# Seven small edits to a one-core encoder step: a later column norm, stored second parts on VectorE, wider biased blocks in the long-range attention, and unit-matrix transposes at the start

## The chip, the cores and the metric

The kernel runs on one core of one Trainium2 chip. The metric is the device time of one execution in microseconds; the kernel before was run three times, and the median counts. Engines are called as the profile calls them: PE (TensorE, the matrix engine), DVE (VectorE), ACT (ScalarE), POOL (GpSimd) and SP (SyncE, which here issues every transfer).

## What is computed

One layer of a streaming encoder, for 2048 prompt tokens and 32 sample tokens of 1024 features, all in float32. The parts that matter here:

```python
qa, ka, va, qb, kb, vb = split_proj(rmsnorm(hp, g_attn[i]), w_in[i])
oa = diff_attn_prompt(qa, ka, va, t5_table, lam)     # 4 heads, two maps each, all earlier keys
ob = band_attn_prompt(qb, kb, vb, band_table[i])     # 8 heads, the last 9 chunks of 64
hp = hp + merge(oa, ob, subln_g[i], out_norm_b[i], w_out[i], lam_init)
hp = ffn_ple(hp, p_prompt[i], g_mlp[i], w_up[i], w_down[i], w_ple_gate[i], w_ple_proj[i])

def diff_core(q, k, v, bias, mask, lam):
    s = jnp.einsum('bqhmd,bkhmd->bhmqk', q, k).astype(jnp.float32) * (HEAD_DIM ** -0.5) + bias[:, None]
    s = jnp.where(mask, s, NEG)
    p = jax.nn.softmax(s, axis=-1)
    w = p[:, :, 0] - lam * p[:, :, 1]
    return jnp.einsum('bhqk,bkhe->bqhe', w.astype(v.dtype), v)

def ffn_ple(h, p, g_mlp, w_up, w_down, w_ple_gate, w_ple_proj):
    c = rmsnorm(h, g_mlp)
    h = h + jnp.square(jax.nn.relu(c @ w_up)) @ w_down
    return h + jax.nn.sigmoid(h @ w_ple_gate) * (p @ w_ple_proj)
```

The bias of the long-range attention differs only for keys less than 128 positions away; further back it is one constant per head, which the kernel subtracts from the table, so that those keys need no bias at all.

## The kernel before

**Numbers in two parts.** Every matrix operand is split into a rounded first part and the rest, its second part (`split`, L181 to L187: the first part by ACT, the second by POOL through `pool_tt`, L166 and L176, or by DVE, L187). `mm3` (L216 to L218) multiplies two such operands with three matmuls. Weights come by `wunit`: one transfer, then a split, by default on ACT and POOL.

**Tokens** go in four blocks of 512 (block 3 has 544, with the samples). `prep` normalises and transposes a block (PE L378 `xp`, ACT L383, DVE L384), `vtile` and `proj` make values, queries and keys (`vps`, `qps`). The order of the stages is: projections of blocks 0 and 1; long-range attention over tiles 0 to 7 (`attn_a` with `JA0`) together with the projections of the band group; band attention (`attn_b`); projections of blocks 2 and 3; long-range attention over tiles 8 to 15 and the samples (`JA1`) together with output projections and the MLP of blocks 0 and 1; then `gate` and `final` of block 1, the output projections of blocks 2 and 3, and the MLP of blocks 2 and 3 in a form with seven products instead of eight (`mlp7`, whose input parts come from `cparts` for block 2 and from `cstage` and `cload`, by way of device memory, for block 3).

**Order.** The program doesn't run in the order in which it is written. A scheduler with a model of the engines fixes, when the program is built, the order of the instructions on each engine; a stage written earlier has priority, and later work fills the gaps. On the chip each engine takes its instructions strictly in that order, so one that waits holds up all behind it. "Filler" below is matmul work of another stage that stands between those of the attention. Generators woven together by `weave` and `weave2` set the written order.

**Long-range attention** (`attn_a_pair`). For each head and pair of tiles of 128 queries, the keys of a tile are cut into blocks: far ones up to 512 wide without bias and a last one of at most 256 with bias. Per block and map: two matmuls into `s` (L633), then for a far block the negated maximum (`nm`, DVE L639), for the last block one DVE operation that adds the bias `ba` and takes the maximum (L642) and a second that turns its sign (L645), then the exponential with its sum on ACT (L647). When there are several blocks, their maxima are brought together (L652 to L659) and the factors `c` of both maps made (L660, L661). ACT multiplies map 1 by its factor (L669) and DVE adds map 0 to it (L670). PE transposes the result (`tpp`, L705), ACT and DVE split it (L712, L713), and PE multiplies it with the values (`o`, L719 to L721). A norm over each head follows: `ss` on PE (L730, L731), then ACT, four steps on POOL (L227 to L231), `os` on DVE (L733) and the store `oT`. The bias tile has one buffer; POOL fills a masked corner of it (L330) once its transfer is there.

**Around block 2's MLP.** The output projection of block 3 (`ops`) is woven with `cparts` of block 2. Its squares are summed on POOL in `sqacc`. Then the gate of block 0 is begun (`hu`: the split of `h`; `gps`, `pps`: its products), and `colnorm` of block 3 follows in the written order: `sh` on ACT, `sl` on DVE, the sums over features on PE (`css`, L1087, L1088), then three ACT and four DVE steps. Its result `r3` is used by `cstage`, which makes the seven input parts of block 3, one eighth for each of the chunks of block 2's MLP from the fifth on, after `final` of block 0 has had four. Of the second parts of an eighth (`cst`) DVE makes all but one, POOL the parts `b11` and `t4`.

Of the kernel before, what the change touches and what calls it, by code (L numbers as in the profile page):

```python
# [13 lines left out]
F32 = mybir.dt.float32  # L14
# [129 lines left out]
class Kern:  # L144
# [125 lines left out]
    def lam(self, cp, wk):  # L270
        nc, a = self.nc, self.a
        lv = wk.tile([P, 4, HD], F32, name="lv")
        for i, n in enumerate(("lambda_q1", "lambda_k1", "lambda_q2", "lambda_k2")):
            self.dma(lv[:, i], a[n].broadcast_to([P, HD]))
        pr = wk.tile([P, 2, HD], F32, name="lpr")
        nc.vector.tensor_tensor(pr[:, 0], lv[:, 0], lv[:, 1], op=ALU.mult)
        nc.vector.tensor_tensor(pr[:, 1], lv[:, 2], lv[:, 3], op=ALU.mult)
        s = wk.tile([P, 2], F32, name="lsum")
        nc.vector.tensor_reduce(s, pr, axis=AX.X, op=ALU.add)
        e = wk.tile([P, 2], F32, name="lexp")  # L280
        nc.scalar.activation(e, s, AF.Exp)
        self.nlam = cp.tile([P, 1], F32, name="nlam")
        nc.vector.tensor_tensor(self.nlam, e[:, 1:2], e[:, 0:1], op=ALU.subtract)
        nc.vector.tensor_scalar(self.nlam, self.nlam, -LAM_INIT, None, op0=ALU.add)
# [40 lines left out]
    def bias_a(self, pool, h):  # L325
        nc = self.nc
        t = pool.tile([P, 256], F32, tag="ba", bufs=1, name="ba")
        src = self.dba[h, 127 : 127 + P * 383].rearrange("(p c) -> p c", c=383)[:, :256]
        self.dma(t, src)
        nc.gpsimd.memset(t[0:64, 192:256], NEG)  # L330
        return t
# [259 lines left out]
    def attn_a_pair(self, g, j, kt, ba, pool, ps_s, ps_t, ps_o):  # L591
# [11 lines left out]
        for qi, t in enumerate(tiles):  # L603
            if samp:
                nr = SS
                blocks = [(SP, PAST + SS, 0)]
# [22 lines left out]
            for bi, (k0, n, near) in enumerate(blocks):  # L629
                for m in range(2):  # L630
# [7 lines left out]
                    if near is None:  # L638
                        nc.vector.tensor_reduce(nmx, s, axis=AX.X, op=ALU.max, negate=True)  # L639
                        src = s  # L640
                    else:
                        nc.vector.tensor_tensor_reduce(  # L642
                            dst, s, ba[:nr, near : near + n], 1.0, -3e38, ALU.add, ALU.max, nmx
                        )
                        nc.vector.tensor_scalar(nmx, nmx, -1.0, None, op0=ALU.mult)  # L645
                        src = dst
                    nc.scalar.activation(dst, src, AF.Exp, bias=nmx, accum_out=z[:nr, m, bi : bi + 1])  # L647
            c = pool.tile([P, 2, 8], F32, tag="c", bufs=2, name="c")
            rz = pool.tile([P, 2], F32, tag="rz", bufs=2, name="rz")
            if nb > 1:  # L650
                gm = pool.tile([P, 2], F32, tag="gm", bufs=2, name="gm")
                nc.vector.tensor_reduce(gm[:nr], nm[:nr, :, :nb], axis=AX.X, op=ALU.min)  # L652
                for m in range(2):
# [6 lines left out]
                nc.vector.tensor_scalar(c[:nr, 0, :nb], c[:nr, 0, :nb], rz[:nr, 0:1], None, op0=ALU.mult)  # L660
                nc.vector.tensor_scalar(  # L661
                    c[:nr, 1, :nb], c[:nr, 1, :nb], rz[:nr, 1:2], self.nlam[:nr], op0=ALU.mult, op1=ALU.mult
                )
            else:
                nc.vector.reciprocal(c[:nr, :, 0], z[:nr, :, 0])
                nc.vector.tensor_scalar(c[:nr, 1, 0:1], c[:nr, 1, 0:1], self.nlam[:nr], None, op0=ALU.mult)
# [363 lines left out]
    def cstage(self, b, up, out, r):  # L1030
# [5 lines left out]
        for k in range(4):  # L1036
# [18 lines left out]
            parts(("b11", "pool"), ("b21", "dve"), ("b22", "dve"))  # L1055
# [5 lines left out]
            parts(("t2", "dve"), ("t1", "dve"), ("t3", "dve"), ("t4", "pool"))  # L1061
# [241 lines left out]
    def gate(self, b, h, up, act, md, wk=None):  # L1303
# [3 lines left out]
        pT = [[up.tile([P, BLK], F32R, tag="u", name="pT") for _ in range(2)] for _ in range(2)]  # L1307
# [14 lines left out]
        for dq in range(2):  # L1322
# [3 lines left out]
            for d4 in range(4):  # L1326
                d = 4 * dq + d4
                wh, wl = self.wunit(Wg[:, P * d : P * d + P].rearrange("(k p) c -> p k c", p=P), [8, P])
                for s0, sn in SUBS[b]:
# [6 lines left out]
                        up.tile([P, BLK], F32, tag="u", name="sig") if wk is None  # L1336
# [29 lines left out]
    def final(self, b, h, up, fk, mm, md=None):  # L1366
# [5 lines left out]
        def side(c0, tn, q):  # L1372
# [8 lines left out]
            if phased and q == 1:  # L1381
                yns[c0, q] = yp
            else:
                yns[c0, q] = up.tile([P, BLK], F32, tag="u", name="yn")[:, :512]
# [4 lines left out]
            junk = up.tile([P, BLK], F32, tag="u", name="junk")[:tn, :512]  # L1389
# [8 lines left out]
        def emit(c0, tn, r):  # L1398
            tt = t0 + c0
            dst = a["y_prompt"][0, tt : tt + tn] if tt < SP else a["y_sample"][0, tt - SP : tt - SP + tn]  # L1400
            for q in range(2):
                src = yn = yns[c0, q]
                if phased and q == 1:
                    yn = up.tile([P, BLK], F32, tag="u", name="yo")[:, :512]
# [24 lines left out]
    def run(self):  # L1429
        tc, nc, a = self.tc, self.nc, self.a  # L1430
        with ExitStack() as top:
# [24 lines left out]
            with ExitStack() as x:  # L1456
# [7 lines left out]
                def first():  # L1464
                    self.consts(cp)

# [4 lines left out]
                units.append(self.vunits(0, 0, pool=wv))  # L1471
                next(gen)
# [136 lines left out]
            r3 = self.colnorm(acc[3][0], 3, 1.0 / D, wk, mm, "mm", None)  # L1609
# [6 lines left out]
            h = box[0]  # L1616
            parts = {}
# [63 lines left out]
```

## Time and profile before

| | us |
|---|---|
| median of three runs | 3172.29 |
| the three runs | 3168.67, 3172.29, 3180.61 |
| profiled execution | 3175.31 |
| its span in the trace | 3173.5 |
| PE busy in the span | 3019.3 (95%) |
| DVE, ACT, POOL busy | 1889.9 (60%), 1878.7 (59%), 1843.7 (58%) |

The profile is of one execution. Busy time is the time in which an engine had at least one instruction under way; PE's matmuls overlap, so the times of single matmuls add up to more than that. In a row of a group, `out<-in` names the tiles (buffer numbers left out), "x768" counts the instructions, then come the total busy time in us, the mean of one in ns, and the idle time of the engine ahead of them with what ended it. A row of the waits reads: engine, tile and line that waited, what ended the wait, us in total, times, longest. A row of the timeline reads: start in us, duration in us, engine, line, operation. A row of the stretches gives, for each window, its length, then the busy time of PE, of PE's weight loads, of DVE, ACT and POOL with the instructions counted, the granted clock of PE as a share, the busy share of the transfer engines and GB/s.

### The profile page before, as it was taken

Reading aid. Unit: us, or ns where it says so; the run is one execution under the profiler, and the core shown is the slowest. Engines: PE = TensorE matmul, PEld = TensorE weight load, DVE = VectorE, ACT = ScalarE, POOL = GpSimd, SP = SyncE. Lnnn points to the kernel's source line nnn. Section 1 sums busy time; section 2 is a strip of 40 time slices with the busy share of each in tenths; the row PEclk is TensorE's granted clock in tenths of the full one; section 3 lists DMA queues with packets and bytes.
Section 4 is the critical chain, followed back from the end, with each engine's and each line's share of the span. In section 5 each row is a group of like instructions: output and inputs, shape, how many; then the busy total and the mean of one; then the engine's idle time right before and its main releaser. Section 6 shows DMA issues by size and latency. Waiting matters only on the chain.

```text
span 3173.5 us, 52785 instructions
## 1 busy us (share of the span) xinstructions
PE 3019.3 (95%) x17913; PEld 2656.2 (84%) x17913; DVE 1889.9 (60%) x4588; ACT 1878.7 (59%) x4166; POOL 1843.7 (58%) x2504
## 2 busy tenths in 40 slices
PE   8999898999999999999999999999799999999998
PEld 7787787899987887878788788878588888999998
DVE  5157774645465654676756656535667775476653
ACT  5257775765676764766666557454555455554545
POOL 2447455332345544655555545677777888767674
PEclk9999999999999999999999999999899999999999
DMA  8788757976788745555663543537433446333231
GB/s 278 243 245 244 206 181 227 261 228 200 211 243 233 210 126 151 155 151 152 173 176 116 141 118 108 160 118 231 129 126 120 151 135 232 122 102 112 87 115 56
DMA packets 522134, 537.17 MB, mean 169 GB/s; under 512 B 38620, under 2 KB 401440, under 8 KB 521864
## 3 DMA queue, kind: packets, MB, share of 16 engines
q1 hardware_dynamic: 521864, 533.80, 57.0%
q8 instruction: 142, 2.33, 0.3%
q14 instruction: 128, 1.05, 0.1%
HBM read 419.88 MB, written 117.75 MB: 169 GB/s over the span
## 4 chain that ended last, share of the span: by engine, by line
PE 68%; DMA 12%; DVE 8%; ACT 4%; POOL 3%; issue 3%; SPq 1%; DVEq 0%; POOLq 0%; ACTq 0%
PE dps L216 6%; PE dps L218 6%; PE ups L216 6%; PE dps L217 6%; PE ups L217 6%; PE ups L218 6%; PE qps L216 3%; PE qps L217 3%; PE qps L218 3%; PE s L633 3%; PE gps L216 2%; PE gps L217 2%; PE gps L218 2%; PE ob L877 2%; PE sb L825 2%
## 5 line engine op out<-in xcount | busy, mean ns | idle before, releaser
L176 POOL TENSOR_TENSOR wl<-wr,wh 128x256 fp32r<-128x256 f32 x648 | 473.1, 762 | 355.2 <-ACT wh L181 332.6
L181 ACT ACTIVATE piece<-wr 128x512 fp32r<-128x512 f32 x406 | 246.4, 625 | 285.8 <-PE ups L217 112.1
L176 POOL TENSOR_TENSOR piece<-wr,piece 128x256 fp32r<-128x256 f32 x404 | 327.0, 835 | 102.0 <-ACT piece L181 93.1
L181 ACT ACTIVATE wh<-wr 128x1024 fp32r<-128x1024 f32 x228 | 241.1, 1058 | 180.2 <-PE qps L217 42.7
L166 POOL TENSOR_TENSOR wl<-wr,wh 128x256 fp32r<-128x256 f32 x264 | 199.7, 787 | 193.7 <-ACT wh L181 187.2
L218 PE MATMUL dps<-uh,piece 128*128 128x272 f32 (+1 forms) x768 | 248.8, 326 | 5.7 <-POOL piece L166 5.6
L216 PE MATMUL dps<-uh,piece 128*128 128x272 f32 (+1 forms) x768 | 246.7, 325 | 5.3 <-ACT piece L181 3.9
L217 PE MATMUL dps<-ul,piece 128*128 128x272 f32 (+1 forms) x768 | 248.2, 324 | 0.0
L216 PE MATMUL ups<-cs,piece 128*128 128x256 f32 (+1 forms) x864 | 246.3, 286 | 1.1 <-DVE r L1219 1.0
L218 PE MATMUL ups<-cs,piece 128*128 128x256 f32 (+1 forms) x864 | 245.5, 284 | 0.0
L217 PE MATMUL ups<-cs,piece 128*128 128x256 f32 (+1 forms) x864 | 245.4, 284 | 0.0
L166 POOL TENSOR_TENSOR piece<-wr,piece 128x256 fp32r<-128x256 f32 x280 | 230.3, 852 | 23.9 <-ACT piece L181 20.9
L216 PE MATMUL qps<-aH,wh 128*128 128x512 f32 (+1 forms) x640 | 232.5, 363 | 7.3 <-ACT kn L506 4.3
L218 PE MATMUL qps<-aH,wl 128*128 128x512 f32 (+1 forms) x640 | 230.3, 360 | 0.0
L217 PE MATMUL qps<-aL,wh 128*128 128x512 f32 (+1 forms) x640 | 229.8, 359 | 0.0
L1208 DVE TENSOR_TENSOR h<-h,dps 128x272 f32<-128x272 f32 (+1 forms) x384 | 189.6, 514 | 58.5 <-PE dps L218 57.8
L1160 DVE TENSOR_TENSOR h<-h,dps 128x512 f32<-128x512 f32 x256 | 174.3, 682 | 78.7 <-PE dps L218 73.5
L216 PE MATMUL dps<-uh,wh 128*128 128x512 f32 x512 | 209.0, 408 | 12.2 <-DVE h L1160 6.9
L633 PE MATMUL s<-ka,q 128*128 128x512 f32 (+3 forms) x768 | 187.4, 345 | 18.4 <-ACT e L647 8.0
L216 PE MATMUL ups<-cH,wh 128*128 128x512 f32 x512 | 203.0, 397 | 1.5 <-ACT cH L181 1.1
L218 PE MATMUL dps<-uh,wl 128*128 128x512 f32 x512 | 202.1, 395 | 0.5 <-POOL wl L166 0.4
L218 PE MATMUL ups<-cH,wl 128*128 128x512 f32 x512 | 201.9, 394 | 0.0
(315 smaller groups left out, 9635.7 us busy)
## 6 DMA issues: line engine op xcount, KB each, us to landing
wr<-w_up SPq DMA_DIRECT2D x128, 512.0 KB, 3.9
wr<-w_down SPq DMA_DIRECT2D x128, 512.0 KB, 3.8
wr<-w_in SPq DMA_DIRECT2D x74, 512.0 KB, 5.4
q<-qS SPq DMA_DIRECT2D x128, 256.0 KB, 5.4
v<-vSa SPq DMA_DIRECT2D x64, 512.0 KB, 3.7
ka<-kS SPq DMA_DIRECT2D x32, 512.0 KB, 8.9
wr<-w_out SPq DMA_DIRECT2D x32, 512.0 KB, 4.7
wr<-w_ple_gate SPq DMA_DIRECT2D x32, 512.0 KB, 4.4
```

The lines of the kernel that those rows point to most:

```text
L166: nc.gpsimd.tensor_tensor(out[:, sl], a[:, sl], b[:, sl], op=op)
L176: nc.gpsimd.tensor_tensor(out[:, sl], a[:, sl], b[:, sl], op=op)
L181: nc.scalar.activation(hi, raw, AF.Copy)
L216: nc.tensor.matmul(ps, lh, rh, start=start and i == 0, stop=False)
L217: nc.tensor.matmul(ps, lh, rl, start=False, stop=False)
L218: nc.tensor.matmul(ps, ll, rh, start=False, stop=stop and i == n - 1)
L633: nc.tensor.matmul(s, q[:, m, hl, P * qi : P * qi + nr], kt[:, m, k0 - kb : k0 - kb + n], start=hl == 0, stop=hl == 1)
L825: ins = nc.tensor.matmul(s, q[:, hl, P * qi : P * qi + nr], kt[:, c : c + w], start=hl == 0, stop=hl == 1)
L877: nc.tensor.matmul(o[:, :, qa:qb], vt, p[:kn, i - kfirst, :, qa:qb], start=x == 0, stop=x == len(order) - 1)
L1160: nc.vector.tensor_tensor(hv, hv, ps, op=ALU.add)
L1208: nc.vector.tensor_tensor(hv, hv, ps, op=ALU.add)
```

## The change

Seven edits:

1. `colnorm` of block 3 moves from ahead of block 2's MLP to behind its first two steps.
2. In `cstage` the second parts of `b11` and `t4` are made by DVE instead of POOL, so that POOL makes none there.
3. In the long-range attention the last, biased block of a tile takes up to 512 keys instead of 256. The bias tile is 512 wide, its first half filled with zeros by POOL. Tiles 2, 3, 6, 7, 10, 11, 14 and 15 have one block fewer.
4. The biased block's operation gives the negated scores and their minimum, so that the separate change of sign goes, and the exponential takes a scale of −1.
5. The factors of both maps are made together, with a vector that holds 1 and −lambda (`lamv`) in place of `nlam`.
6. PE transposes the unit matrix 14 times once it is written, and 20 times behind the first tile's transposes. The results aren't used.
7. In `gate` and `final` the tiles of the pool `up` take the pool's width (`up.aw`, 512 for blocks 0 and 1) instead of 544.

```diff
     def bias_a(self, pool, h):
         nc = self.nc
-        t = pool.tile([P, 256], F32, tag="ba", bufs=1, name="ba")
+        t = pool.tile([P, 512], F32, tag="ba", bufs=1, name="ba")
+        nc.gpsimd.memset(t[:, :256], 0.0)
         src = self.dba[h, 127 : 127 + P * 383].rearrange("(p c) -> p c", c=383)[:, :256]
-        self.dma(t, src)
-        nc.gpsimd.memset(t[0:64, 192:256], NEG)
+        self.dma(t[:, 256:], src)
+        nc.gpsimd.memset(t[0:64, 448:512], NEG)
         return t
...
-                nfar = max(nkeys - 256, 0)
+                nfar = max(nkeys - 512, 0)
...
-                blocks.append((nfar, nkeys - nfar, 256 - (nkeys - nfar)))
+                blocks.append((nfar, nkeys - nfar, 512 - (nkeys - nfar)))
...
                     if near is None:
                         nc.vector.tensor_reduce(nmx, s, axis=AX.X, op=ALU.max, negate=True)
-                        src = s
+                        nc.scalar.activation(dst, s, AF.Exp, bias=nmx, accum_out=z[:nr, m, bi : bi + 1])
                     else:
                         nc.vector.tensor_tensor_reduce(
-                            dst, s, ba[:nr, near : near + n], 1.0, -3e38, ALU.add, ALU.max, nmx
+                            dst, s, ba[:nr, near : near + n], -1.0, 3e38, ALU.add, ALU.min, nmx
                         )
-                        nc.vector.tensor_scalar(nmx, nmx, -1.0, None, op0=ALU.mult)
-                        src = dst
-                    nc.scalar.activation(dst, src, AF.Exp, bias=nmx, accum_out=z[:nr, m, bi : bi + 1])
+                        nc.scalar.activation(
+                            dst, dst, AF.Exp, bias=nmx, scale=-1.0, accum_out=z[:nr, m, bi : bi + 1]
+                        )
...
                 nc.vector.reciprocal(rz[:nr], rz[:nr])
-                nc.vector.tensor_scalar(c[:nr, 0, :nb], c[:nr, 0, :nb], rz[:nr, 0:1], None, op0=ALU.mult)
-                nc.vector.tensor_scalar(
-                    c[:nr, 1, :nb], c[:nr, 1, :nb], rz[:nr, 1:2], self.nlam[:nr], op0=ALU.mult, op1=ALU.mult
+                nc.vector.tensor_tensor(rz[:nr], rz[:nr], self.lamv[:nr], op=ALU.mult)
+                nc.vector.tensor_tensor(
+                    c[:nr, :, :nb], c[:nr, :, :nb], rz[:nr].unsqueeze(2).broadcast_to([nr, 2, nb]), op=ALU.mult
                 )
...
-            parts(("b11", "pool"), ("b21", "dve"), ("b22", "dve"))
+            parts(("b11", "dve"), ("b21", "dve"), ("b22", "dve"))
...
-            parts(("t2", "dve"), ("t1", "dve"), ("t3", "dve"), ("t4", "pool"))
+            parts(("t2", "dve"), ("t1", "dve"), ("t3", "dve"), ("t4", "dve"))
...
                 def first():
                     self.consts(cp)
+                    busy(14)
+
+                def busy(n):
+                    t = ps_o.tile([P, 512], F32, tag="o", name="busy")
+                    for _ in range(n):
+                        nc.tensor.transpose(t[:, :P], self.ident, self.ident)
...
                 next(gen)
                 units.append(self.vunits(0, 0, pool=wv))
+                busy(20)
                 next(gen)
...
             g = self.gate(0, h, up, None, md, wk)
             next(g)
-            r3 = self.colnorm(acc[3][0], 3, 1.0 / D, wk, mm, "mm", None)
             box = []
             m = self.mlp7(2, hh[1], box, ops[2], wk, up, mm, md)
             weave(g, self.along(iter(range(3)), m), 1)
...
             h = box[0]
+            r3 = self.colnorm(acc[3][0], 3, 1.0 / D, wk, mm, "mm", None)
             parts = {}
             weave(m, chain(f, self.cstage(3, up, parts, r3)), 1)
```

More of the change, by code (lines that the diff above doesn't have):

```diff
@@ L281, in lam @@
         nc.scalar.activation(e, s, AF.Exp)
-        self.nlam = cp.tile([P, 1], F32, name="nlam")
-        nc.vector.tensor_tensor(self.nlam, e[:, 1:2], e[:, 0:1], op=ALU.subtract)
-        nc.vector.tensor_scalar(self.nlam, self.nlam, -LAM_INIT, None, op0=ALU.add)
+        self.lamv = cp.tile([P, 2], F32, name="lamv")
+        nc.gpsimd.memset(self.lamv, 1.0)
+        nlam = self.lamv[:, 1:2]
+        nc.vector.tensor_tensor(nlam, e[:, 1:2], e[:, 0:1], op=ALU.subtract)
+        nc.vector.tensor_scalar(nlam, nlam, -LAM_INIT, None, op0=ALU.add)
     def biases(self, wk, ps):
@@ L605, in attn_a_pair @@
                 nr = SS
-                blocks = [(SP, PAST + SS, 0)]
+                blocks = [(SP, PAST + SS, 256)]
                 kb = SP
@@ L1306, in gate @@
         Wg, Wp = a["w_ple_gate"][0], a["w_ple_proj"][0]
-        pT = [[up.tile([P, BLK], F32R, tag="u", name="pT") for _ in range(2)] for _ in range(2)]
+        pT = [[up.tile([P, up.aw], F32R, tag="u", name="pT") for _ in range(2)] for _ in range(2)]
         for i in range(2):
```

12 lines of the change are left out of this document (6 added, 6 removed).

## The prediction

> **What bounds the kernel now.** I read the busy times by stage first, then the list of what PE (the matrix engine) waited for, then the timeline at single places. The stages are: the start (0 to 40 us), the first long-range attention part (183 to 483), the hand-over to band attention (483 to 640), the second long-range part inside the MLP of blocks 0 and 1 (1190 to 2040), the gap after the last output projection (2231 to 2256), the stretch with `cstage` (2455 to 2650), and the end.
>
> ```profile
> core 0: us, PE busy (x) PEld busy (x) DVE busy (x) ACT busy (x) POOL busy (x), PEclk, DMA share, GB/s
> 0.00:40.00 40.00, 27.93 (x199) 25.18 (x200) 24.65 (x83) 33.06 (x96) 19.95 (x35) 1.00 1.02 308
> ...
> 183.00:483.00 300.00, 272.46 (x1665) 240.43 (x1666) 216.27 (x716) 214.00 (x637) 166.21 (x239) 0.94 0.75 215
> 483.00:640.00 157.00, 140.28 (x853) 123.92 (x852) 85.78 (x321) 105.69 (x254) 71.86 (x119) 0.94 0.87 250
> ...
> 1190.00:2040.00 850.00, 824.19 (x4171) 691.74 (x4170) 517.87 (x1150) 530.86 (x1222) 473.25 (x673) 0.99 0.51 142
> ...
> 2231.00:2256.00 25.00, 2.65 (x9) 1.75 (x8) 21.34 (x34) 12.89 (x32) 16.52 (x20) 0.59 0.66 226
> ...
> 2455.00:2650.00 195.00, 187.28 (x1149) 164.82 (x1148) 146.38 (x224) 100.01 (x194) 161.35 (x184) 1.00 0.48 156
> 2650.00:3174.00 524.00, 508.18 (x3773) 491.91 (x3771) 303.00 (x592) 273.85 (x520) 354.61 (x453) 0.99 0.35 112
> ```
>
> PE is nearly always busy, so only its idle time can be won: 27.5 us (300 − 272.5) in the first long-range part, 16.7 in the hand-over, 25.8 in the second part, 22.3 in the gap, 7.7 beside `cstage`. The change takes next to no work from PE: the 128 score matmuls that go are merged into wider ones over the same columns.
>
> ```profile
> PE css L1087 <- ACT sh L181: 20.9, 1, 20.9
> PE s L633 <- ACT e L647: 8.0, 10, 2.9
> ...
> PE dps L218 <- POOL piece L166: 5.6, 10, 1.1
> ```
>
> One wait stands out, the column norm's 20.9 us; the next are 8 us and less, in many pieces.
>
> **Long-range chain.** The blocks with a bias grow from 256 to 512 columns, so tiles 2, 3, 6, 7, 10, 11, 14 and 15 of each head lose one block for both maps. The sign change (L645) goes into the bias operation, and the factors are multiplied in one operation for both maps.
>
> ```profile
> L639 DVE TENSOR_REDUCE nm<-s 128x1 f32<-128x512 f32 x104 | 70.0, 683 | 26.6 <-PE s L633 26.0
> L639 DVE TENSOR_REDUCE nm<-s 128x1 f32<-128x384 f32 x128 | 69.1, 550 | 52.5 <-PE s L633 52.2
> L642 DVE CUSTOM_DVE_ANT_0 e<-s,ba 128x256 f32<-128x256 f32 x120 | 49.2, 417 | 42.7 <-PE s L633 41.1 <-POOL ba L330 1.0
> L645 DVE TENSOR_SCALAR nm<-nm 128x1 f32<-128x1 f32 x128 | 18.1, 147 | 1.1
> ...
> L660 DVE TENSOR_SCALAR c<-c,rz 128x2 f32<-128x2 f32 (+3 forms) x56 | 20.0, 357 | 1.0
> L661 DVE TENSOR_SCALAR c<-c,rz,nlam 128x2 f32<-128x2 f32 (+3 forms) x56 | 24.8, 443 | 0.0
> ...
> L647 ACT ACTIVATE e<-s,nm 128x384 f32<-128x384 f32 x128 | 74.2, 584 | 34.9 <-DVE nm L639 29.9 <-DVE e L670 5.1
> L647 ACT ACTIVATE e<-s,nm 128x512 f32<-128x512 f32 x104 | 70.9, 684 | 30.5 <-DVE nm L639 24.1 <-DVE e L670 6.1
> L647 ACT ACTIVATE e<-e,nm 128x256 f32<-128x256 f32 x120 | 60.8, 508 | 37.3 <-DVE nm L645 36.9
> L647 ACT ACTIVATION_READ_ACCUMULATOR e<-s,nm 128x1 f32 x256 | 52.0, 203 | 0.0
> ```
>
> DVE (VectorE): L645 goes, −18. Reductions fall from 104 to 80 at 512 columns and from 128 to 88 at 384: 24 × 0.683 + 40 × 0.550 = −38. Of 120 biased blocks of 256 columns, 8 stay, 8 become 384 and 104 become 512 wide; 512 isn't shown. From 0.417 us and the slope of the reductions (133 ns for 128 columns) I estimate 0.55 and 0.68 us: +29. L660 and L661, 44.8 us, become 96 short products, between 0.147 us (L645) and 0.357 us (L660) each, 14 to 34 us; I take 24, so −21. Sum −48 us of 734. ACT (ScalarE): −40 × 0.584 − 24 × 0.684 − 64 accumulator reads × 0.203 = −53; the wide biased blocks by the same slope (0.78 ns a column) +22; sum −31 of 745. Some multiplications fall away besides; I leave them out.
>
> In each part that is about 40 us less on the two engines between which the chain alternates, and the 36.9 us that ACT waited for L645 go. Two tiles are in flight, so about half, 20 us, shortens the attention. But filler leaves with it: in the built order the first part ends with 66 fewer 256-column filler matmuls ahead of its end, the second with 354 fewer of 512. They must run later, so only PE's idle time is won. Such matmuls start 0.115 us apart:
>
> ```profile
> 14.51 0.28 PE L216 MATMUL vps<-wh,aH 128*128 128x256 f32 x1
> 14.62 0.28 PE L217 MATMUL vps<-wl,aH 128*128 128x256 f32 x1
> ```
>
> **First part**: 20 us less 66 × 0.115 leaves 12; I take −9, bounds 0 and −27.5. **Second part**: PE is 97% busy and the displaced work runs where PE also idles 3% (15.8 of 524), so I take −5, bounds 0 and −13, half its idle time.
>
> **Hand-over.** Between the first part's last `ss` and the first band matmul, the order had 100 matmuls of 512 columns; now it has 66 of 256 and 4 of 512.
>
> ```profile
> 481.61 0.28 PE L730 MATMUL ss<-sh,ones_r 128*128 128x256 f32 x1
> ...
> 488.12 0.74 POOL L227 TENSOR_TENSOR rsv<-rsv,rsy 128x256 f32<-128x256 f32 x1
> ...
> 500.76 0.73 POOL L231 TENSOR_TENSOR rsy<-rsy,rsv 128x256 f32<-128x256 f32 x1
> ...
> 502.96 0.60 SPq L157 DMA_DIRECT2D oT<-os  x1
> ...
> 514.81 0.97 PE L825 MATMUL sb<-kbt,q 128*128 128x128 f32 x6
> ```
>
> The norm on POOL (GpSimd) took 13.4 us from L227 to L231, because weight splits stood between its four steps; in the new order they follow each other, about 2.6 us at 0.7 us a step. So the way of 33 us shortens to some 22. Today 100 × 0.23 us of filler leave a hole of 10; in the new order 66 × 0.115 + 4 × 0.23 and one tile's transposes (1.4) make 10 us of work, and the hole is 12. +2; bounds −3 and +12, the whole hole new. Band attention gets the moved 96 matmuls as filler: −2 (0 to −4).
>
> **Stored second parts.** Eight operations move from POOL to DVE.
>
> ```profile
> L187 DVE TENSOR_TENSOR cst<-ct,cst x20: 426/974/1015, 2466.5 to 2620.6; 128x272 fp32r<-128x272 f32 x20
> ...
> L166 POOL TENSOR_TENSOR cst<-ct,cst x8: 764/1030/1252, 2463.4 to 2619.7; 128x272 fp32r<-128x272 f32 x8
> ...
>   DVE ct L1042: 7.9, 8
> ```
>
> POOL loses 8 × 1.03 us and the 7.9 us for which it stood before them with the weight splits queued behind; DVE gains 8 × 0.97, to 154 of 195 us. The PE idle in this stretch is 7.7 us, partly "POOL piece". −3, bounds 0 and −6.
>
> **Column norm of block 3.** It moves behind two steps of block 2's MLP.
>
> ```profile
> 2252.42 0.82 PE L1087 MATMUL css<-sh,ones_r 128*128 128x272 f32 x2 [20.95 <-ACT sh L181]
> ...
> 2254.78 0.63 ACT L181 ACTIVATE hu<-h 128x512 fp32r<-128x512 f32 x1
> ...
> 2255.46 0.79 PE L216 MATMUL gps<-hu,piece 128*128 128x512 f32 x1 [1.38 <-ACT hu L181]
> ```
>
> The 20.9 us don't go: PE's next work needs `hu`, which ACT makes, and ACT still has `sh` (to 2252.4) ahead of it in the new order. `hu` starts there instead of at 2254.78, so −2.4, and the four norm matmuls later cost 0.5: −2 (bounds −1 and −2.4). The norm's result is wanted only four chunks later.
>
> **Transposes of the unit matrix** stand on PE ahead of the first tile (14) and behind it (20).
>
> ```profile
> 1.11 0.37 POOL masks.py:199 TENSOR_SCALAR_AFFINE_SELECT ident<-ident 128x128 f32<-128x128 f32 x1
> ...
> 4.53 1.94 PE L378 MATMUL xp<-ident,x 128*128 128x128 f32 x8 [4.53 <-DMA x<-x_prompt]
> ...
> 8.22 0.58 PE L216 MATMUL vps<-wh,aH 128*128 128x256 f32 x1 [1.74 <-ACT wh L181]
> ...
> 18.20 1.35 PE L378 MATMUL xp<-ident,x 128*128 128x128 f32 x8
> ```
>
> A transpose costs 0.24 us at 4.5 us and 0.17 us at 18: PE starts slow, though the granted clock reads 1.00. Fourteen from 1.5 end at 4.9. If they make PE fast, the tile (1.35) and the 20 (3.4) end at 9.6, the first projection 1.4 us late, and what follows gains: 0.07 us on each of the next 8 transposes and as much on some 16 matmuls, about 2 us. If they don't, 1.94 + 4.85 bring it to 11.7, 3.5 us late. ACT is the busiest engine here (33 of 40 us); I take 0, bounds −2 and +3.5. The Trainium skill ("TensorE: Matmul & The Clock Gate", Part 4: PE-mode transpose) says that transposes don't count as activity for the clock. By that rule the late end would hold; no transpose-only stretch of this trace tests it.
>
> **Sum.** −9 − 5 + 2 − 2 − 3 − 2 + 0 = −19 us. The profiled execution took 3175.3 us (span 3173.5 and 1.8 around it), so 3156; the runs' median, 3172.3, lies 3.0 lower: I predict 3154. A measurement of this kernel tells about 0.5% from no change, that is 3156.4 to 3188.2.
>
> **Rivals.**
> 1. *The idle time only moves.* The displaced filler brings its holes along, and attention gives nothing: −3 − 2 and the hand-over's +2, about 3169. For it: PE is already 97% busy in the second part. Chance 0.23.
> 2. *The chain sets the attention's length*, and its idle time goes mostly: −18 and −12 instead of −14, about 3138. For it: DVE and ACT are each above 70% busy in the first part. Chance 0.10.
> 3. *The transposes stay slow* and delay the start by 3.5 us: 3157. Chance 0.07; by the skill's rule it would be the likelier of the two.
> 4. *Slower: the new fill of the bias tile holds POOL.* It waits at each head's start until the head before has let go of the one buffer, ahead of weight splits.
>
> ```profile
> L330 POOL MEMSET ba<- x16: 141/144/146, 175.9 to 1900.4; 64x64 f32 x16
> ...
>   DMA ba<-dba: 29.6, 10
> ```
>
> The sixteen fills themselves cost little, at 0.14 us for 64 columns and half the rows some 0.3 us each. Today's ten waits last 3.0 us each. If all 16 double, POOL loses 48 us; if half reaches PE, 3178. It decides from 1.2 us a head that reaches PE (19 / 16). Against it: POOL is 55% busy there and almost no PE wait in these stages names it. Chance 0.08.
>
> **Chances.** Forecast 0.52, own range 3146 to 3160, some 0.40 of it below 3156.4. Faster by over 0.5%: 0.40 + 0.10 = 0.50. Within: 0.12 + 0.23 + 0.07 + 0.02 = 0.44. Slower: 0.06. The range 3136 to 3178 takes in rivals 2 and 4.
>
> **What would show it.** Right: idle of PE in both long-range parts down by 9 and 5 us; the first projection no later than 10 us; the wait at 2231 moved to `hu` and still about 20 us; fewer "POOL piece" waits beside `cstage`. Wrong: a PE hole over 15 us before the first band matmul; POOL waits at L330 far above 30 us; DVE's wide biased block well over 0.7 us; ACT's `hu` behind other work.

## The result and the profile after

| | before | after |
|---|---|---|
| median, us (14 runs each) | 3170.74 | 3176.76 |
| the runs, us | 3168.05 to 3180.61 | 3171.39 to 3184.15 |
| profiled execution, us | 3175.31 | 3175.05 |

The ratio is 1.0021, with an interval of 1.0013 to 1.0029: no faster, by the medians 6 us slower, where the forecast had 19 us less. The measured time lies within the 0.5% of no change and within the range, but on the other side of no change. The two profiled executions are of one length only because before's lay 4.6 us above its median and after's 1.7 below; a single profile here can't show a difference of 6 us, only where time moved.

The stretches are cut at the same events in both kernels: first score matmul, last `ss` of the first long-range part, first band matmul, first `ups`, last `ss`, first `gps` of block 1. The stretches of before:

```profile
core 0: us, PE busy (x) PEld busy (x) DVE busy (x) ACT busy (x) POOL busy (x), PEclk, DMA share, GB/s
183.40:481.60 298.20, 271.05 (x1657) 239.14 (x1658) 215.75 (x714) 213.23 (x635) 164.71 (x236) 0.94 0.76 216
481.60:514.80 33.20, 27.32 (x115) 21.60 (x114) 12.33 (x29) 14.05 (x31) 24.17 (x38) 0.90 0.84 251
514.80:1048.60 533.80, 511.45 (x3261) 460.18 (x3260) 299.73 (x1038) 357.34 (x760) 218.74 (x338) 0.98 0.80 229
1048.60:2031.10 982.50, 954.87 (x4837) 800.38 (x4836) 596.54 (x1423) 629.34 (x1427) 533.83 (x760) 0.99 0.52 145
2031.10:2073.70 42.60, 40.79 (x177) 32.74 (x176) 27.95 (x36) 21.43 (x34) 34.89 (x47) 1.00 0.82 261
...
2231.20:2255.50 24.30, 1.95 (x8) 1.08 (x6) 21.17 (x33) 12.27 (x30) 15.82 (x20) 0.58 0.67 230
```

And of after:

```profile
187.40:463.70 276.30, 252.81 (x1518) 222.68 (x1519) 198.02 (x551) 195.15 (x522) 166.73 (x243) 0.94 0.79 225
463.70:482.10 18.40, 12.71 (x87) 11.45 (x85) 8.01 (x21) 7.64 (x21) 4.62 (x9) 0.81 0.65 184
482.10:1060.30 578.20, 548.62 (x3436) 488.12 (x3437) 317.62 (x1117) 386.08 (x822) 234.69 (x368) 0.98 0.79 228
1060.30:1946.50 886.20, 856.85 (x4350) 720.28 (x4349) 547.27 (x1225) 578.27 (x1275) 489.59 (x694) 0.99 0.53 148
1946.50:2074.10 127.60, 122.23 (x530) 98.57 (x529) 44.00 (x64) 50.09 (x70) 85.03 (x123) 1.00 0.48 150
...
2231.80:2253.50 21.70, 0.27 (x3) 0.04 (x2) 20.87 (x33) 10.96 (x26) 16.10 (x19) 0.62 0.79 263
...
2455.00:2650.00 195.00, 187.09 (x1153) 165.39 (x1152) 150.88 (x232) 99.85 (x194) 154.72 (x178) 1.00 0.49 157
```

Read the lengths first. Both long-range parts did get shorter: the first by 22 us, the hand-over by 15, and the last `ss` came 85 us earlier, at 1946. And block 1's gate (its first `gps`) still starts at 2074. All that was won is spent in the stretches behind: band attention and its neighbours last 44 us longer, the MLP alone 128 instead of 43. Then read PE's idle time (length less busy): 27.2 → 23.5, 5.9 → 5.7, 22.4 → 29.6, 27.6 → 29.4, 1.8 → 5.4. In sum 84.8 → 93.5: it went up by 9 where the forecast had it 14 lower. How far one execution can be trusted is shown by five kernels of the experiments below that have before's order of matmuls up to the gate (e3, e4, e7, e11, e13). Their idle time in these stretches is 84.0 to 85.5 us in sum, so the rise is no scatter. From the first score matmul to the gate they take 1884.7 to 1888.9 us, before's own profile 1890.3 and after's 1886.7, so this length didn't change: the 14 us that the forecast took off it are missing in full.

What PE waited for:

```profile
PE gps L216 <- ACT hu L181: 21.4, 1, 21.4
PE sb L828 <- DVE stb L831: 9.6, 8, 3.3
...
PE dps L218 <- POOL piece L166: 5.9, 9, 1.1
```

The big wait now stands at `hu`; "POOL piece" is as before (5.6), and band attention's own scores (`sb`, from 4.4) wait longer. ACT's wait in the biased block, first in before (where L645 is the sign change), then in after (where L645 is the bias operation):

```profile
ACT e L647 <- DVE nm L645: 51.9, 42, 3.7
```

```profile
ACT e L648 <- DVE nm L645: 50.0, 44, 3.6
```

The sign change has gone, and the wait hasn't: it now ends with the bias operation. The softmax groups (mean ns behind the comma):

```profile
L645 DVE CUSTOM_DVE_ANT_0 e<-s,ba 128x512 f32<-128x512 f32 x104 | 70.8, 685 | 36.5 <-PE s L636 30.1 <-PE tpp L708 4.6 <-PE qps L217 1.2
L642 DVE TENSOR_REDUCE nm<-s 128x1 f32<-128x512 f32 x80 | 54.0, 684 | 17.4 <-PE s L636 17.2
...
L642 DVE TENSOR_REDUCE nm<-s 128x1 f32<-128x384 f32 x88 | 47.6, 549 | 36.0 <-PE s L636 35.9
```

The counts are the predicted ones, the wide biased block costs 0.685 us (0.68 estimated). DVE's total went from 1889.9 to 1851.8 us, ACT's from 1878.7 to 1861.3.

### The profile page after: what moved, and what is told of

Its sections match the earlier page's. It is cut to its first block, busy times and chain, and to the rows that moved or that the text cites. A ratio compares the mean times of both kernels' runs of the same rounds, so it can differ in the third digit from the quotient of the medians.

```text
span 3173.3 us, 52271 instructions
## 1 busy us (share of the span) xinstructions
PE 3013.2 (95%) x17819; PEld 2651.7 (84%) x17819; DVE 1851.8 (58%) x4332; ACT 1861.3 (59%) x3990; POOL 1838.5 (58%) x2513
## 5 line engine op out<-in xcount | busy, mean ns | idle before, releaser
L176 POOL TENSOR_TENSOR piece<-wr,piece 128x256 fp32r<-128x256 f32 x404 | 327.5, 838 | 101.9 <-ACT piece L181 84.8
L217 PE MATMUL ups<-cL,wh 128*128 128x512 f32 x512 | 201.7, 394 | 0.0
L217 PE MATMUL dps<-ul,wh 128*128 128x512 f32 x512 | 201.5, 393 | 0.0
```

The source lines that it names most:

```text
L176: nc.gpsimd.tensor_tensor(out[:, sl], a[:, sl], b[:, sl], op=op)
L217: nc.tensor.matmul(ps, lh, rl, start=False, stop=False)
```

## Experiments: the parts by themselves

All ratios are to the kernel before, run beside each experiment on the same chip, with 95% intervals. Before's median lay between 3167.2 and 3175.1 us in these sets of runs, so compare the ratios and not the times. "Marks" are the times of single events in the profiles. Edit 6 alone:

```diff
                 def first():
                     self.consts(cp)
+                    busy(14)
...
                 units.append(self.vunits(0, 0, pool=wv))
+                busy(20)
                 next(gen)
```

> The kernel before with only the 34 transposes of the unit matrix added. Theory 1 (the transposes hold PE past the first projection, and the start is late by what the changed kernel's first query projection shows, 73.5 against 70.3 us): 3 to 4 us slower, first query projection near 73.5, and the delay stays to the end because PE is full behind it. Rival (the start is bound by ACT and transfers, and the late start is taken up by idle time before 183 us): within 1 us of before, first long-range score within 1 us of 183.4.

3197.5 us, 1.0068 (1.0055 to 1.0081), 22 us slower. The marks tell where: the first `qps` comes 3.5 us late, the last one 2.8 early, block 1's gate 15.8 late. So the loss isn't at the start; e12 and e13 below take it up.

Edits 3 to 5 without edit 7:

```diff
-        t = pool.tile([P, 256], F32, tag="ba", bufs=1, name="ba")
+        t = pool.tile([P, 512], F32, tag="ba", bufs=1, name="ba")
...
-                nfar = max(nkeys - 256, 0)
+                nfar = max(nkeys - 512, 0)
```

> The kernel before with only the three edits of the long-range attention (512-wide biased block, sign in the bias operation, factors together). Theory 1 (PE's idle time in the attention stages only moves, since the filler that leaves the stage takes its holes along): within 3 us of before, with the attention's end some 80 us earlier and block 1's gate at the same time as before within 3 us. Rival A (the chain's saved time is won): 10 to 15 us faster. Rival B (the new order of the filler costs: in the changed kernel the first output projection is 9.6 us late and the MLP 11.7 us late): 4 to 8 us slower.

3505.8 us, 1.1038 (1.1023 to 1.1053). The second long-range part ran nearly alone; the stretch up to its end (1688.9) and the one behind:

```profile
1067.00:1688.90 621.90, 427.20 (x1907) 329.81 (x1905) 372.12 (x994) 382.78 (x993) 93.81 (x164) 0.73 0.42 111
1688.90:2403.30 714.40, 695.88 (x2973) 557.71 (x2973) 207.56 (x295) 260.51 (x352) 468.10 (x653) 0.99 0.37 114
```

```profile
L181 ACT ACTIVATE uh<-relu x64: 611/632/641, 1691.0 to 2385.9; 128x512 fp32r<-128x512 f32 x64
```

The last line is the tile `uh` of blocks 0 and 1, which lies in the pool `uq`: its first use waits until attention has ended. The wide bias tile takes 1,024 bytes a partition more; `uq` has 8 buffers, and 544 → 512 columns gives back 8 × 32 × 4 = 1,024. Edit 7 looks like nothing but a width. It is the room for edit 3, and with it the 330 us are gone (e6).

Edit 2 alone, and edit 1 alone:

```diff
-            parts(("b11", "pool"), ("b21", "dve"), ("b22", "dve"))
+            parts(("b11", "dve"), ("b21", "dve"), ("b22", "dve"))
...
-            parts(("t2", "dve"), ("t1", "dve"), ("t3", "dve"), ("t4", "pool"))
+            parts(("t2", "dve"), ("t1", "dve"), ("t3", "dve"), ("t4", "dve"))
```

```diff
             next(g)
-            r3 = self.colnorm(acc[3][0], 3, 1.0 / D, wk, mm, "mm", None)
...
             h = box[0]
+            r3 = self.colnorm(acc[3][0], 3, 1.0 / D, wk, mm, "mm", None)
```

> The kernel before with only the two second parts of the staging moved from POOL to DVE. Theory 1 (POOL's queue isn't what ends PE's waits there, DVE's takes their place): within 1 us of before; PE idle from 2455 to 2650 stays near 7.7 us. Rival (POOL's 16 us in this stretch were what PE waited for): 3 us faster, PE idle there 4 to 5 us.

> The kernel before with only the column norm of block 3 moved. Both theories of the gap: PE's idle time at 2231 stays at about 20 us and now ends with ACT's hu; the gate's first product comes 2.0 to 2.6 us earlier. Theory 1: the gain holds to the end, 2 us faster. Rival (the norm's DVE and ACT work, moved into block 2's MLP, gives the gain back before 2725 us): within 1 us of before.

3171.4 us, 0.9990 (0.9981 to 0.9999), and 3171.5 us, 0.9992 (0.9980 to 1.0004). In e3, PE's idle time beside `cstage` was 8.1 us for 7.7. In e4 the time from the last `ops` to the first `gps` was 21.0 us instead of 24.3, but the time from there to the last `gps` with `hu` was 2.4 us longer. Both diffs together:

> Edits 1 and 2 together, no other; the built order of the matrix engine is that of before up to the last output projection. Each alone measured 0.999 and 0.9992. Theory: they add up, 3169 us, ratio 0.998 +- 0.001, the fastest of all versions so far. Rival: the 2 to 3 us that the norm wins at the gap are given back before 2726 us, as in the run of edit 1 alone, and the second parts win nothing: ratio 0.9995 to 1.0005.

1.0006 (0.9997 to 1.0015): the two edits don't add up to a gain. Edit 7 alone, with the built order of before, shows how well that is known:

```diff
-        pT = [[up.tile([P, BLK], F32R, tag="u", name="pT") for _ in range(2)] for _ in range(2)]
+        pT = [[up.tile([P, up.aw], F32R, tag="u", name="pT") for _ in range(2)] for _ in range(2)]
```

> Edit 7 alone: four tiles of the gate and the last stage take 512 instead of 544 columns. The built order of every engine is that of before. Theory: nothing, 3175 us, ratio 1.000 +- 0.001, which also tells how far two kernels with one order lie apart. [...]

1.0007 (0.9997 to 1.0017), with the same instructions in the same order on PE, DVE, ACT and POOL as in before's profile. Effects of 0.1%, that of e3 among them, are at the edge of what these runs tell.

## Experiments: the attention

With room, that is the diffs of e2 and e7 together (edits 3, 4, 5 and 7):

> Attention edits 3 to 5 together with edit 7, the narrower pool of the gate and the last stage; nothing else changed. If the wide bias block failed by itself in the earlier run only because the MLP's pools no longer fitted beside attention, the MLP starts again beside the second long-range part and the time is 3160 to 3185 us. Theory 1 (the idle time only moves): 3175 us, ratio 1.000 +- 0.0015, with the second long-range part ending some 85 us earlier and block 1's gate at the same time as before. Theory 2 (attention wins the 14 us of the forecast and something else in the change loses them): 3161 us, ratio 0.9955. If room was not the cause: about 3500 us again.

3174.9 us, 1.0014 (1.0004 to 1.0024), with the last `ss` 83 us earlier and block 1's gate at 2076.6: theory 1, the idle time only moves. Then its halves, the shorter chain alone (edits 4 and 5, first diff) and the wide block alone (the diffs of `bias_a` and `nfar` above, and edit 7):

```diff
-                            dst, s, ba[:nr, near : near + n], 1.0, -3e38, ALU.add, ALU.max, nmx
+                            dst, s, ba[:nr, near : near + n], -1.0, 3e38, ALU.add, ALU.min, nmx
...
-                        nc.vector.tensor_scalar(nmx, nmx, -1.0, None, op0=ALU.mult)
```

> Only edits 4 and 5: the sign goes into the bias operation and the factors are multiplied together; the bias block stays 256 wide. VectorE loses 128 sign changes (18 us) and some 21 us of factor products, ScalarE its 36.9 us of waits for the sign, spread over both long-range parts; no score matmul changes. Theory 1 (the idle time of the matrix engine only moves): ratio 0.9995 to 1.0005, 3175 us. Theory 2 (a shorter chain shortens attention, a third of the 39 us reaches the end): 3162 us, ratio 0.996. Rival 3 (the order built anew is worse by chance, as with the transposes): 1.002 or more.

> Only edit 3, the bias block up to 512 columns wide, with the narrower pool of edit 7 that gives it room; the sign change and the factor products stay as before. 128 score matmuls go; the profiles of before and after show that the score matmuls of the same columns then take 13 us less of the matrix engine (196.5 to 183.2 us). Theory 1 (what attention saves turns into idle time of the matrix engine): 3175 us, ratio 1.000 to 1.002. Theory 2 (saved work of the matrix engine reaches the end, and the short chain of edits 4 and 5 is what costs it again): 3162 us, ratio 0.996.

1.0011 (1.0001 to 1.0020) and 1.0019 (1.0008 to 1.0030). Neither wins. In e8, DVE lost 14.9 us of work (1875.1), but ACT's wait didn't go: it ends with the bias operation and lasts 54.5 us in sum, for 51.9. Every mark after the start lies within 2.5 us of before's. The first long-range part takes 295.7 us in e8 and 279.8 in e9; in before's order it takes 294.8 to 298.2 over six profiles. So what shortens attention is the wide block and not the shorter chain. The opposite of e8:

```diff
-nc.vector.tensor_scalar(nmx, nmx, -1.0, None, op0=ALU.mult)
+for _ in range(3):
+    nc.vector.tensor_scalar(nmx, nmx, -1.0, None, op0=ALU.mult)
```

> The kernel before with the sign change made three times instead of once, so the chain between VectorE and ScalarE gets 256 operations of 0.147 us more (38 us on VectorE) and ScalarE some 74 us more of waits for the sign, the opposite of edit 4 and twice as large. Theory 1 (the order fills the holes of attention with other work, so the chain's length between its present ends does not reach the end): 3175 to 3180 us, ratio 1.000 to 1.0015. Theory 2 (the chain sets the attention's length and with it the end): half of the 74 us at least, 3210 us, ratio 1.011 or more.

3198.1 us, 1.0082 (1.0069 to 1.0094): both numbers miss. The first long-range part with its hand-over grew by 30 us, and by the last `qps` 22 of the 31 at its end had been won back: projections had been drawn into the longer part. At the end 20 were left by the profile, 26 by the ratio. The built order of PE is another from the first score matmuls on, so this run doesn't tell what the longer chain costs from what its order costs. A longer chain did lengthen attention; a shorter one (e8) shortened nothing.

Is PE's work what reaches it? One of the three value matmuls left out (the product with the second part of the values: 256 matmuls of 256 columns and a few small ones; the output lacks that term), in before and with the attention edits:

```diff
 nc.tensor.matmul(oo, v[:kn, x, 0], pH[...], start=first, stop=False)
-nc.tensor.matmul(oo, v[:kn, x, 0], pL[...], start=False, stop=False)
-nc.tensor.matmul(oo, v[:kn, x, 1], pH[...], start=False, stop=last)
+nc.tensor.matmul(oo, v[:kn, x, 0], pL[...], start=False, stop=last)
```

> The kernel before with one of the three value matmuls of long-range attention left out (the product with the second part of v: 256 matmuls of 256 columns and 16 smaller ones); nothing waits on it alone. At 0.115 us from start to start that is 29 us of the matrix engine's work. Theory 1 (saved work of the matrix engine reaches the end): 3146 us, ratio 0.9905 to 0.993. Theory 2 (it becomes idle time, because attention waits for VectorE and ScalarE anyway): 3170 to 3175 us, ratio 0.998 to 1.000.

> Attention edits with room (3, 4, 5 and 7, which measured 1.0014) with the same third of the value matmuls left out as in the run of before that measured 0.9939. Theory 1 (in the shortened attention the matrix engine waits for other engines, so saved work there becomes idle time): ratio 0.998 to 1.001. Theory 2 (saved work is worth the same in both, and what the wide block does not win lies in its built order): 0.9953, some 19 us less than 1.0014.

0.9939 (0.9926 to 0.9951), and 0.9942 (0.9930 to 0.9955) against e6's 1.0014: 19 and 23 us of the 29. Each has a built order of its own, but the two agree: two thirds and more of PE's saved work reaches the end. So PE stays the bound, and attention's holes don't eat what is saved. Then why do the merged score matmuls win nothing, when their busy time, added up width by width, fell from 196 to 183 us? They are cut in two again in e14:

```diff
+two = near is not None and not samp and t % 4 > 1
+for c0, c1 in ((0, n - 256), (n - 256, n)) if two else ((0, n),):
     for hl in range(2):
         nc.tensor.matmul(s[:, c0:c1], q[...], kt[:, m, k0 - kb + c0 : k0 - kb + c1], ...)
```

> Attention edits with room (edits 3, 4, 5 and 7), but the score matmuls of the wide bias blocks of tiles 2, 3, 6, 7, 10, 11, 14 and 15 are cut in two again, so there are as many as before (768); VectorE and ScalarE work on wide blocks as in the change. Theory 1 (the merged matmuls win 13 us and the shorter attention, with its displaced work, costs that much): 3190 us, ratio 1.005 to 1.007. Theory 2 (the merged matmuls are worth nothing at the end, because the matrix engine's saved time becomes idle time): as with the merged ones, 3175 to 3180 us, ratio 1.000 to 1.002.

3169.8 us, 0.9997 (0.9988 to 1.0006): as many matmuls as before, and if anything less time than merged (1.0014), though in another built order. So the 13 us don't show as time that PE got back. Starts in after, of 512 columns:

```profile
1950.24 0.39 PE L217 MATMUL ups<-cL,wh 128*128 128x512 f32 x1
1950.47 0.39 PE L218 MATMUL ups<-cH,wl 128*128 128x512 f32 x1
1950.70 0.39 PE L216 MATMUL ups<-cH,wh 128*128 128x512 f32 x1
```

They follow each other at 0.23 us, those of 256 in the prediction's rows at 0.115: a column costs the same. Only the recorded duration (0.39 against 0.28) doesn't halve, so merging lowers the sum of the durations without setting PE free. The busy time is another matter. From the first score matmul to the gate, in before, in after and in e14:

```profile
183.40:2073.70 1890.30, 1805.48 (x10041) 1554.03 (x10042) 1152.29 (x3240) 1235.40 (x2885) 976.34 (x1416) 0.98 0.65 184
```

```profile
187.40:2074.10 1886.70, 1793.21 (x9913) 1541.10 (x9914) 1114.92 (x2977) 1217.23 (x2709) 980.65 (x1434) 0.98 0.64 184
```

```profile
185.90:2065.70 1879.80, 1792.03 (x10041) 1545.20 (x10042) 1114.35 (x2976) 1214.57 (x2709) 984.47 (x1433) 0.98 0.64 185
```

PE's busy time is 12 us lower in after, but just as low in e14, which has all of before's matmuls. So merging is not what lowered it, and what did stays open. It also means that the 9 us more of idle time aren't 9 us lost: with the same columns to work on, PE was busy for less and idle for more in the same length. What stands is the length, which didn't fall. The whole change cut in the same way, without the transposes:

> The whole change without the transposes (edits 1 to 5 and 7), with the score matmuls of the wide blocks cut in two as in the run that measured 0.9997. The order of the matrix engine is that run's up to block 3's norm. Theory 1 (edits 1 and 2 win nothing at the end): ratio 0.9990 to 1.0005, the time of before. Theory 2 (they win their 2 to 5 us here): 0.998 to 0.9985, the first version faster than before.

3167.7 us, 0.9996 (0.9986 to 1.0005). It is the best form of the whole change, and level with before. No version that computes everything is clearly faster than before.

## Experiments: the transposes and the order

Within the full change the transposes cost nothing:

> The changed kernel without the 34 transposes of the unit matrix (edits 1 to 5 and 7 stay). Past its first 2600 or so matrix instructions the built order is that of the changed kernel. Theory 1 (inside the full change the transposes cost only their own time at the start, 3.5 us there as the first query projection showed, and nothing of it is won back): 3173 us, ratio to before 1.001. Theory 2 (they cost what they cost alone, 20 us): 3157 us, ratio 0.995. Theory 3 (the late start is made up by 1060 us, so they cost nothing): 3177 us, ratio 1.002.

The diff is that of e1 turned back. 3178.4 us, 1.0023 (1.0011 to 1.0035), as with them (1.0021): theory 3. The first `qps` comes at 70.0 us without them and at 73.5 with them, the last at 920.2 and 911.5: whatever the start loses is won back by then. The two built orders differ up to about 500 us. Why 20 us when alone? Only the first fourteen, then only eleven, in the kernel before:

```diff
                     self.consts(cp)
+                    busy(14)
```

```diff
                     self.consts(cp)
+                    busy(11)
```

> The kernel before with only the first 14 of the 34 transposes, those that run before the first tile has come. The matrix engine's built order is then, but for some 500 lines, that of the run with all 34, which took 3197 us. Theory 1 (the order that comes out is what costs; the transposes themselves are done before the first tile): 3190 to 3200 us, ratio 1.005 to 1.007. Theory 2 (the time of the transposes after the first tile is what costs): 3175 us, ratio 1.000 +- 0.001.

> The kernel before with 11 transposes ahead of the first tile, three fewer than in the run that took 3194 us. With 11 the built order of the matrix engine is that of before, with 14 it is another in most of its length. Theory 1 (the built order costs the 20 us): 3175 us, ratio 0.999 to 1.001. Theory 2 (transposes at the start cost by themselves, by the clock or by what they delay): 11/14 of 20 us, 3190 us, ratio 1.005.

1.0065 (1.0053 to 1.0077) and 1.0004 (0.9995 to 1.0013). Three transposes of a fifth of a microsecond make 19 us, because between eleven and fourteen the scheduler builds another order for most of PE's program: e12's matmuls follow e1's order behind the start, and e13's follow before's from 11.1 us on. The stretch from the first `ups` to block 1's gate, in e1 and then in e13:

```profile
1045.70:2089.50 1043.80, 1003.94 (x5068) 843.96 (x5067) 631.79 (x1501) 665.16 (x1488) 574.55 (x809) 0.98 0.53 149
```

```profile
1045.50:2068.70 1023.20, 992.71 (x5014) 830.92 (x5014) 622.42 (x1459) 650.32 (x1460) 569.49 (x806) 0.99 0.53 150
```

In e1's order 54 more matmuls stand in this stretch and PE idles 39.9 us in it instead of 30.5. Which order the scheduler falls into is worth as much as the whole forecast of 19 us.

## Why the prediction was wrong, step by step

- **PE bounds, only its idle time can be won.** Right: two thirds and more of the work taken from PE reached the end (e15, e17).
- **"The change takes next to no work from PE."** Right, by the distance between starts, against the recorded durations.
- **The chain's sizes.** Right in sum for DVE: −38 us in all, of which the second parts added some 8, so −46 in attention for −48. The factors came to 30.0 us, not 24, and the multiplications left out (L670, 134.5 → 125.5) made up for it. ACT: −17 for −31, because rows of one line overlap: the four rows of L647 add up to 257.9 us, while the whole line covers 248.9.
- **"The 36.9 us that ACT waited for L645 go … about half, 20 us, shortens the attention."** The wait didn't go (51.9 → 50.0 over all widths; the forecast's 36.9 are the 256-wide blocks). The first part did become 22 us shorter (298.2 → 276.3; 18.5 against the shortest profile of before's order). But most of that came from the wide block (279.8 in e9), and the shorter chain alone did nothing (295.7 in e8). So the 20 is right in part by luck.
- **"First part … I take −9", "second part … I take −5".** This step failed. It took the shortening, less the filler that leaves with it, as idle time won, and with the hand-over and the band filler the sum had 14 us off the time from the first score matmul to block 1's gate. That time is 1886.7 us, within the 1884.7 to 1890.3 of before's order. Idle time fell by 3.7 in the first part and not at all in the second. When attention shortened, filler left with it, and where it went PE idled too: the band stretch idles 5.1% (29.6 of 578.2 us; before 4.2%), and the MLP alone 4.2% (5.4 of 127.6), more than the MLP beside attention (3.3%, 29.4 of 886.2). The forecast had the band stretch gain 2 us and the MLP alone lose nothing. Rival 1 was the better forecast, and still too kind.
- **Hand-over and "band filler −2".** The way of 33 us became 18 (22 forecast), the norm on POOL 2.9 us from L227's start, 468.45, to L231's end, 471.34 (2.6 forecast). The hole stayed (5.9 to 5.7); the forecast's hole of 10 was worked out from 100 starts, while the trace of before had only 5.9 us idle there. The band stretches didn't lose 2 us of idle time, they gained 7.2.
- **Stored second parts −3.** POOL's busy time beside `cstage` fell by 6.6 and DVE's rose by 4.5, yet PE's idle time there is 7.9 for 7.7: POOL's delay was not what PE waited for.
- **Column norm −2.** Right at its place (24.3 → 21.7, and `hu` does stand behind `sh`); given back before 2726 us in the run of edit 1 alone (e4), where the ratio can't be told from 1.
- **Transposes 0, bounds −2 and +3.5.** Inside the change the bounds held at the end (e5). At the start its fast case came true: the 20 ended at 7.9 us, and the first projection came at 8.95, not at 9.6. Alone the transposes cost 22 us, far outside the bounds, because these counted only what stands beside the start and not the order that is built from it.
- **What wasn't seen.** Edit 7 is what makes edit 3 possible; it was given no line in the sum.
- **The sum.** 3175.3 − 19 − 3.0 is 3153, not 3154; nothing hangs on it.

Rival 4, the fill of the bias tile holding POOL, did not happen. The fills in after, and what POOL waited for ahead of them:

```profile
L330 POOL MEMSET ba<- x16: 308/314/332, 175.6 to 1814.7; 128x256 f32 x16
...
  DVE nm L645: 10.7, 4
```

They take 0.31 us each (0.3 forecast) and held POOL four times, 10.7 us in all. The wait for the bias transfer, ahead of the masked corner, stayed (28.6 us for 29.6).

By the marks of the two profiled executions the balance is +4.0 us at the first score matmul, −3.6 from there to block 1's gate, −2.4 by `hu`'s first product and +1.8 behind it: nothing. Where the 6 us of the medians are lost, these two profiles don't show.

What stays open: four built orders with the wide block measure 1.0014, 1.0019, 1.0021 and 1.0023, two with its matmuls cut 0.9997 and 0.9996. Whether the cut itself or the orders that came with it make the 0.2%, no run tells apart. In the two that are cut (e14, e16) something was won ahead: 1879.8 and 1882.1 us from the first score matmul to the gate, for 1884.7 and more in before's order. From the gate to the end they take 1104.3 and 1103.5 us, for 1099.0 to 1100.3, and so give most of it back.

## What to carry to other kernels

In this kernel one engine is busy 95% and a scheduler fills the holes of the rest, and shortening another engine's chain moved work, not the end; ask for each stage where its filler goes and how much the bound engine idles there. Ask of a wait that an edit is to remove what it will end with instead. Judge work of a pipelined engine by the distance between starts, not by summed durations. An edit as small as three transposes can tip a built order: compare the orders before laying a loss to the operation itself, and look for the memory that a pool gives back before calling an edit nothing.

## What the runs showed of the hardware

**Transposes alone can make PE fast.** The start in after (34 transposes), then in e12 (14) and e13 (11):

```profile
1.55 3.25 PE L1474 MATMUL busy<-ident 128*128 128x128 f32 x14 [1.55 <-POOL ident masks.py:199]
4.59 1.15 PE L381 MATMUL xp<-ident,x 128*128 128x128 f32 x8
5.58 2.35 PE L1474 MATMUL busy<-ident 128*128 128x128 f32 x20
8.95 0.38 PE L216 MATMUL vps<-wh,aH 128*128 128x256 f32 x1 [1.03 <-ACT aH L386]
```

```profile
4.59 1.92 PE L378 MATMUL xp<-ident,x 128*128 128x128 f32 x8
9.18 0.58 PE L216 MATMUL vps<-wh,aH 128*128 128x256 f32 x1 [2.68 <-ACT aH L383]
```

```profile
4.57 1.97 PE L378 MATMUL xp<-ident,x 128*128 128x128 f32 x8 [0.41 <-DMA x<-x_prompt]
8.80 0.58 PE L216 MATMUL vps<-wh,aH 128*128 128x256 f32 x1 [2.27 <-ACT wh L181]
```

With 34, the first projection's matmul takes 0.38 us, otherwise 0.58, and the 20 follow at 0.12 us each where the first fourteen took 0.23. So a stretch of transposes alone does make PE fast here (e1's profile shows the same 0.38). The Trainium skill ("TensorE: Matmul & The Clock Gate", Part 4: PE-mode transpose) says that transposes don't engage the fast clock; these rows speak against it. How many it takes isn't shown: in after PE is fast from the first tile's eight on (1.15), that is behind fourteen (1.10 in e1), while in e12 the eight are slow (1.92) with the same fourteen ahead. These are single executions, and why they differ stays open.

**The granted clock dips after the start**, in after and in e7:

```profile
10.00:20.00 10.00, 7.41 (x35) 6.62 (x35) 6.57 (x28) 7.64 (x29) 4.19 (x7) 0.66 1.03 342
20.00:30.00 10.00, 8.70 (x59) 8.32 (x60) 8.97 (x30) 8.02 (x26) 5.61 (x8) 0.83 1.04 318
```

```profile
20.00:30.00 10.00, 8.05 (x50) 7.44 (x49) 7.06 (x23) 9.13 (x29) 5.62 (x8) 0.66 1.08 336
```

e7 has no transposes and before's order, and before's own profile reads 1.00 there. Its first `qps` is 2.2 us later than before's, after's 3.2. Over the fifteen profiles of kernels without transposes the first `qps` comes at 70.0 to 74.4 us, so after's 73.5 is no proof of a delay by the transposes: the dip comes with and without them.

**Where PE had holes, its clock was low.** Where PE was busy 69% (e2's stretch above: 427 of 622 us) the granted clock was 0.73; in the gap at 2232, 0.62; in the stretches at 97% busy, 0.99. The low clock costs where matmuls run: in e2's stretch a third of the 256-column matmuls that waited for nothing (150 of 447) started about 0.21 us behind the one ahead, where 0.12 is usual. In before's second part it is 30 of 520. That holes bring the low clock about is a reading of these stretches; no run changed one without the other.
